# Norm factors of q and k as one power on GpSimd, and rope, factors and sums of squares over all four token blocks in one instruction

## The chip, the cores and the metric

The kernel runs on one core of a Trainium2 chip. The metric is device time in microseconds (us) of one execution. The engines are called by the short names of the profile: PE (TensorE, matrix products), PEld (its weight loads), DVE (VectorE), ACT (ScalarE), POOL (GpSimd) and SP (SyncE, which issues the DMAs here). They run at the same time, each with its own queue of instructions, in the order in which that queue was written.

## The reference

One block of a sparse-attention and recurrent network, followed by two layers of a second block. All arithmetic is in fp32, with 512 tokens and a width of 1024. What matters here is the second block: in each of its two layers four attention mixers read the same normed input, and each normalises its queries and keys head by head before the scores are formed.

```
def rms_norm(x, g):
    xf = x.astype(jnp.float32)
    y = xf * lax.rsqrt(jnp.mean(xf * xf, axis=-1, keepdims=True) + EPS)
    return (y * g.astype(jnp.float32)).astype(x.dtype)

def apply_rope(x, ang):
    x1, x2 = xf[..., :half], xf[..., half:]
    return jnp.concatenate([x1 * cos - x2 * sin, x1 * sin + x2 * cos], axis=-1)

# in each layer, between two feed-forward parts:
ya = neighbourhood_mixer(...)   # q, k: 4 heads of 64
yb = mla_mixer(...)             # q, k: 4 heads of 96 (64 plain + 32 with rope)
yc = diff_mixer(...)            # q, k: 8 halves of 32
yd = gqa_mixer(...)             # q: 4 heads of 64, k: 2 heads of 64, axial rope on both
x = x + jnp.concatenate([ya, yb, yc, yd], axis=-1) @ w_out[l]
```

The first block normalises the queries of its four head groups in the same way.

## The kernel before

Matrix products are done in three passes (L142 to L144, L172 to L174): each operand is split into a high and a low part, high by a copy on ACT (L125 for weights), low by a subtraction (L127 for weights, L225 for activations). In the attention stages the low part of the weights is made on POOL, elsewhere on DVE.

The program runs as one sequence of stages: the first block's attention and recurrence (`nsa`, about the first 500 us), feed-forward layers, the mixers of layer 0 (`mix`, about 1400 to 1740 us), feed-forward layers, the mixers of layer 1 (about 2460 to 2790 us), and a last feed-forward layer. Inside `mix` the sixteen heads run as a pipeline, in the order of mixers C (`diff`), A (`na`), D (`gqa`), B (`mla`): for head i the probabilities times values (`pv`), for head i+1 scores and softmax (`soft`), for head i+2 the transposes (`prep`). A filler (`Fill`) hands out the projections of the next mixer and the output products of earlier ones in small steps between these.

The final order on each engine is not that of the code: a scheduler with a simulated timeline orders the instructions by priority, and the steps of the filler have a lower one. Each engine then works through its queue strictly in order.

For q and k of a mixer the steps on the way from projection to transposes are:

- `proj` and `to` put the product into `tq` or `tk` (tokens on partitions, four blocks of 128 tokens side by side, `tb` is the block);
- `sums` (L677) squares it on ACT into a scratch tile `sqp` of 512 columns, of which there are two, and adds up each head on DVE (L683), one pair of instructions for each block;
- `factors` (L686) turns the sums of squares `hs` into reciprocal roots: with more than one head by `rstd_v` (L191), three Newton steps on DVE, with a single one by `rstd` (L182), one scaled sum on DVE and one power on POOL (L188);
- `bcm` (L699) multiplies q or k by the factors on DVE, block by block;
- `rope_n` (L690) makes two products with the tables on POOL (L693, L694) and adds the swapped halves of each 32 columns on DVE (L697), block by block; L1188 spreads the rotated part of `mla`'s k over the heads.

The names that return below: `hs` sums of squares, `nm` their scaled mean, `nt` the scratch of the Newton steps, `rq`, `rk` the factors, `sqp` scratch, `box` the q and k of `mla`, `ry` the factors of a mixer's output norm, `P` probabilities, `st` row statistics of the softmax, `PTl` the low part of the transposed probabilities, `nab` and `E` the bias of `na`.

Of the kernel before, what the change touches and what calls it, by code (L numbers as in the profile page):

```python
# [84 lines left out]
class Kern:  # L85
# [96 lines left out]
    def rstd(self, ss, width, n, tag, bufs=2):  # L182

        nc = self.nc
        m = self.sm.tile([128, n], FT, tag=tag + "m", name=tag + "m", bufs=bufs)
        nc.vector.tensor_scalar(m, ss, 1.0 / width, EPS, op0=OP.mult, op1=OP.add)
        r = self.sm.tile([128, n], FT, tag=tag, name=tag, bufs=bufs)
        nc.gpsimd.tensor_tensor(r, m, self.mhalf[:, :n], op=OP.pow)  # L188
        return r

    def rstd_v(self, ss, width, n, tag, bufs=2):  # L191

        V = self.nc.vector
        m, t = (self.sm.tile([128, n], FT, tag=c, name=c, bufs=2) for c in ("nm", "nt"))
        r = self.sm.tile([128, n], FT, tag=tag, name=tag, bufs=bufs)
        V.tensor_scalar(m, ss, 1.0 / width, EPS, op0=OP.mult, op1=OP.add)
        V.tensor_scalar(r.bitcast(I32), m.bitcast(I32), -0.5, 1597463007.0, op0=OP.mult, op1=OP.add)
        for _ in range(3):
            V.scalar_tensor_tensor(t, r, -0.5, r, op0=OP.mult, op1=OP.mult)
            V.tensor_mul(t, t, m)  # L200
            V.scalar_tensor_tensor(r, t, 1.5, r, op0=OP.add, op1=OP.mult)
        return r
# [426 lines left out]
    def mix(self, px, l, norm):  # L629
# [44 lines left out]
        def sqp():  # L674
            return tl("sqp", [128, T], FT, 2)

        def sums(t, n, d):  # L677

            ss = small("hs", [4, n], 4)
            for tb in range(4):  # L680
                sv = sqp()[:, :n * d].rearrange("p (h d) -> p h d", d=d)
                S.activation(sv, t[:, tb], AF.Square)
                V.tensor_reduce(ss[:, tb], sv, axis=AX, op=OP.add)  # L683
            return ss

        def factors(ss, n, d, tag):  # L686
            f = self.rstd_v if n > 1 else self.rstd
            return f(ss.rearrange("p t n -> p (t n)"), d, 4 * n, tag, 4).rearrange("p (t n) -> p t n", n=n)

        def rope_n(rope, t, tb, n, d):  # L690

            a = sqp()[:, :n * d].rearrange("p (h d) -> p h d", d=d)
# [183 lines left out]
        def diff():  # L876
# [19 lines left out]
            def projs():  # L896
                yield from proj(w_c[0], 256, to(q))
                rq = factors(sums(q8, 8, 32), 8, 32, "rq2")
                for tb in range(4):
                    bcm(q8[:, tb], rq[:, tb], 8, 32)  # L900
                yield from proj(w_c[1], 256, to(k))
                rk = factors(sums(k8, 8, 32), 8, 32, "rk2")
                for tb in range(4):
                    bcm(k8[:, tb], rk[:, tb], 8, 32)
                yield from proj(w_c[2], 256, lambda tb, ps, rt: vevac(Vt[:, tb], v4(ps), rt))
# [74 lines left out]
        def gqa():  # L980
            rope = tl("rope", [128, 2, 2, 4, 64])
# [14 lines left out]
            def post(t, n, i):  # L996
                th = t.rearrange("p t (h d) -> p t h d", d=64)
                f = factors(sums(th, n, 64), n, 64, "rq2")
                for tb in range(4):
                    bcm(th[:, tb], f[:, tb], n, 64)  # L1000
                    rope_n(rope[:, i], th[:, tb], tb, n, 64)
# [33 lines left out]
        def na():  # L1035
# [11 lines left out]
            def post(t):  # L1047
                th = t.rearrange("p t (h d) -> p t h d", d=64)
                f = factors(sums(th, 4, 64), 4, 64, "rq2")
                for tb in range(4):  # L1050
                    bcm(th[:, tb], f[:, tb], 4, 64)
# [78 lines left out]
        def mla():  # L1130
# [20 lines left out]
            def projs():  # L1151
# [33 lines left out]
                for tb in range(4):  # L1185
# [18 lines left out]
                for tb in range(4):  # L1204
                    bcm(qm[:, tb], rq[:, tb], 4, 96)
                    rope_n(rope[:, 0], qm[:, tb, :, 64:96], tb, 4, 32)
# [91 lines left out]
    def nsa(self, pa, pl, attnT, lru):  # L1298
# [176 lines left out]
        def post_q(g, t):  # L1475
# [6 lines left out]
            rq = self.rstd_v(ss, 64, 16, "rq")  # L1482
# [341 lines left out]
```

## Time and profile before

| | us |
|---|---|
| median of 3 runs | 3163.69 (3162.76 to 3170.32) |
| the profiled execution, its own time | 3163.88 |
| its span, first to last instruction | 3162.1 |
| PE busy in the span | 3041.4 (96%) |
| DVE busy | 1797.1 (57%) |
| ACT busy | 1396.7 (44%) |
| POOL busy | 686.8 (22%) |

The time of the profiled execution is 1.8 us above its span (what lies around the first and the last instruction) and 0.2 us above the median, so sums made in the trace can be read as sums of the median. Shares over the whole span are averages of stages that differ: in the feed-forward stages PE is busy without a gap and DVE about half of the time, while in the mixers DVE is nearly full. So the views that count here are those by stretch. A number in brackets behind a row of a timeline is the time that the engine sat idle before it, with the instruction that ended the wait.

### The profile page before, as it was taken

What the parts mean: (1) busy time and instruction counts of PE and PEld (TensorE: products, weight loads), DVE (VectorE), ACT (ScalarE), POOL (GpSimd) and SP (SyncE); (2) the same over time, 40 slices, a digit from 0 to 9 for tenths busy, and PEclk for the clock granted to TensorE, in tenths of its full rate; (3) what the DMA queues carried; (4) which work ended last, traced back from release to release, by engine and by line L of the source; (5) the groups of instructions that cost most, each with busy time, mean ns of one, the idle gap of its engine ahead of it and who ended that gap; (6) DMA issues with size and microseconds to landing.
All of it is one profiled execution on the core that took longest, in us unless ns stands there. A gap on an engine that the chain in (4) does not pass through costs nothing.

```text
span 3162.1 us, 41620 instructions
## 1 busy us (share of the span) xinstructions
PE 3041.4 (96%) x15289; PEld 2554.9 (81%) x15289; DVE 1797.1 (57%) x3520; ACT 1396.7 (44%) x2753; POOL 686.8 (22%) x746
## 2 busy tenths in 40 slices
PE   7999999999999999999888999999999998999998
PEld 6888777878888888888866888888888987778886
DVE  7677675454443444438886554354443698664433
ACT  4577674343332333336664333333332666543322
POOL 3366640010000000025752000010001566310000
PEclk9999999999999999999999999999999998999999
DMA  4221112333233233333201323323233322123332
GB/s 146 90 64 54 54 34 79 116 121 99 95 97 97 94 100 97 97 111 94 79 28 40 100 94 100 97 90 100 94 97 97 110 77 58 34 80 98 96 100 80
DMA packets 105268, 275.84 MB, mean 87 GB/s; under 512 B 27172, under 2 KB 36900, under 8 KB 104904
## 3 DMA queue, kind: packets, MB, share of 16 engines
q1 hardware_dynamic: 105064, 273.18, 27.8%
q8 instruction: 120, 1.97, 0.3%
q14 instruction: 84, 0.69, 0.1%
HBM read 268.93 MB, written 6.80 MB: 87 GB/s over the span
## 4 chain that ended last, share of the span: by engine, by line
PE 80%; DVE 10%; ACT 3%; POOL 2%; issue 2%; DMA 1%; SPq 0%; DVEq 0%; POOLq 0%; ACTq 0%
PE ps_mm L142 8%; PE ps_mm L144 8%; PE ps_mm L143 8%; PE ps_s L143 7%; PE ps_s L144 7%; PE ps_s L142 7%; PE ps_t L144 7%; PE ps_t L143 7%; PE ps_t L142 7%; PE ps_mm L172 2%; PE ps_mm L173 2%; PE ps_mm L174 2%; DVE PTl L225 1%; PE ps_t L1591 1%; DVE st L774 1%
## 5 line engine op out<-in xcount | busy, mean ns | idle before, releaser
L125 ACT ACTIVATE hi<-raw 128x512 fp32r<-128x512 f32 (+2 forms) x952 | 595.5, 627 | 1342.8 <-PE ps_mm L143 402.9
L127 DVE TENSOR_TENSOR lo<-raw,hi 128x512 fp32r<-128x512 f32 x782 | 543.6, 697 | 932.5 <-ACT hi L125 925.2
L142 PE MATMUL ps_mm<-xh,hi 128*128 128x512 f32 (+1 forms) x792 | 311.5, 394 | 2.8 <-ACT hi L125 2.3
L144 PE MATMUL ps_mm<-xh,lo 128*128 128x512 f32 (+1 forms) x792 | 309.7, 393 | 3.1 <-POOL lo L127 3.1
L143 PE MATMUL ps_mm<-xl,hi 128*128 128x512 f32 (+1 forms) x792 | 310.0, 391 | 0.0
L238 POOL TENSOR_TENSOR acc<-acc,sq 128x512 f32<-128x512 f32 x49 | 72.7, 1483 | 1056.4 <-ACT sq L236 529.4
L142 PE MATMUL ps_s<-xh,hi 128*128 128x512 f32 x656 | 253.2, 392 | 7.4 <-ACT hi L125 7.4
L143 PE MATMUL ps_s<-xl,hi 128*128 128x512 f32 x656 | 257.2, 392 | 2.3 <-DVE xl L243 2.1
L172 PE MATMUL ps_mm<-hi,xh 128*128 128x256 f32 (+1 forms) x896 | 256.2, 289 | 1.2 <-DVE gz L466 0.9
L144 PE MATMUL ps_s<-xh,lo 128*128 128x512 f32 x656 | 256.1, 391 | 0.0
L173 PE MATMUL ps_mm<-lo,xh 128*128 128x256 f32 (+1 forms) x896 | 255.1, 287 | 0.0
L127 POOL TENSOR_TENSOR lo<-raw,hi 128x512 fp32r<-128x512 f32 (+2 forms) x170 | 223.1, 1316 | 147.1 <-ACT hi L125 134.8
L174 PE MATMUL ps_mm<-hi,xl 128*128 128x256 f32 (+1 forms) x896 | 254.2, 287 | 0.1
L144 PE MATMUL ps_t<-xh,lo 128*128 128x512 f32 x608 | 236.3, 390 | 1.8 <-DVE lo L127 1.7
L142 PE MATMUL ps_t<-xh,hi 128*128 128x512 f32 x608 | 236.8, 390 | 0.0
L143 PE MATMUL ps_t<-xl,hi 128*128 128x512 f32 x608 | 236.6, 389 | 0.0
L144 PEld LDWEIGHTS ps_mm<-xh,lo 128*128 128x128 f32 (+1 forms) x792 | 148.7, 188 | 35.3 <-POOL lo L127 4.1
L142 PEld LDWEIGHTS ps_mm<-xh,hi 128*128 128x128 f32 (+1 forms) x792 | 148.9, 188 | 34.8 <-ACT hi L125 2.6
L172 PEld LDWEIGHTS ps_mm<-hi,xh 128*128 128x128 f32 x896 | 173.0, 194 | 3.1 <-DVE gz L466 1.1
L173 PEld LDWEIGHTS ps_mm<-lo,xh 128*128 128x128 f32 x896 | 173.2, 194 | 1.8 <-issue 0.4
L143 PEld LDWEIGHTS ps_mm<-xl,hi 128*128 128x128 f32 (+1 forms) x792 | 149.0, 188 | 30.6
L174 PEld LDWEIGHTS ps_mm<-hi,xl 128*128 128x128 f32 x896 | 172.1, 194 | 2.0 <-DVE xl L243 0.5
(540 smaller groups left out, 6714.4 us busy)
## 6 DMA issues: line engine op xcount, KB each, us to landing
raw<-in_w_g SPq DMA_DIRECT2D x110, 512.0 KB
raw<-in_w_u SPq DMA_DIRECT2D x110, 512.0 KB
raw<-in_w_d SPq DMA_DIRECT2D x108, 512.0 KB
raw<-in_w_o SPq DMA_DIRECT2D x24, 512.0 KB
raw<-in_w_c SPq DMA_DIRECT2D x16, 512.0 KB
raw<-in_w_m SPq DMA_DIRECT2D x16, 512.0 KB
raw<-in_w_a SPq DMA_DIRECT2D x12, 512.0 KB
raw<-in_w_d SPq DMA_DIRECT2D x20, 256.0 KB
```

Of the source, the lines that this page charges most:

```text
L125: nc.scalar.activation(hi[:, :c], x, AF.Copy)
L127: eng.tensor_tensor(lo[:, :c], x, hi[:, :c].bitcast(FT), op=OP.subtract)
L142: mm(ps, wh, mh(km), start=s, stop=False)
L143: mm(ps, wh, ml(km), start=False, stop=False)
L144: mm(ps, wl, mh(km), start=False, stop=e)
L172: mm(out[tb], h, wh, start=k == 0 and tb % 2 == 0, stop=False)
L173: mm(out[tb], h, wl, start=False, stop=False)
L174: mm(out[tb], o, wh, start=False, stop=k == K - 1 and tb % 2 == 1)
L225: self.nc.vector.tensor_sub(lo, src, hi.bitcast(FT))
L238: nc.gpsimd.tensor_tensor(acc, acc, sq, op=OP.add)
L774: V.tensor_reduce(mn, ps, axis=AX, op=OP.max, negate=True)
L1591: PE.transpose(tps[:, (qb - kb) * 128:(qb - kb + 1) * 128], P[qb][:, kb * 128:kb * 128 + 128], ident)
```

## The change

The Newton steps are gone: every factor comes from `rstd`, that is one scaled sum on DVE (L186) and one power on POOL (L188), whose width is the number of factors: 32 columns for `diff`'s q and k, 16 for those of `na`, for `gqa`'s q, `mla`'s q and k and the first block's q, 8 for `gqa`'s k. The scratch of the scaled sum becomes one tile name, `nm`, with four buffers for all callers. `sums`, `bcm` and `rope_n` work over as many token blocks at once as fit into 512 columns of scratch (`bcm` over all four).

```
     def rstd(self, ss, width, n, tag, bufs=2):
...
-        m = self.sm.tile([128, n], FT, tag=tag + "m", name=tag + "m", bufs=bufs)
+        m = self.sm.tile([128, 32], FT, tag="nm", name="nm", bufs=4)[:, :n]
         nc.vector.tensor_scalar(m, ss, 1.0 / width, EPS, op0=OP.mult, op1=OP.add)
         r = self.sm.tile([128, n], FT, tag=tag, name=tag, bufs=bufs)
         nc.gpsimd.tensor_tensor(r, m, self.mhalf[:, :n], op=OP.pow)
-        return r
-
-    def rstd_v(self, ss, width, n, tag, bufs=2):
-        V.tensor_scalar(m, ss, 1.0 / width, EPS, op0=OP.mult, op1=OP.add)
-        V.tensor_scalar(r.bitcast(I32), m.bitcast(I32), -0.5, 1597463007.0, op0=OP.mult, op1=OP.add)
-        for _ in range(3):
-            V.scalar_tensor_tensor(t, r, -0.5, r, op0=OP.mult, op1=OP.mult)
-            V.tensor_mul(t, t, m)
-            V.scalar_tensor_tensor(r, t, 1.5, r, op0=OP.add, op1=OP.mult)
         return r
...
         def sums(t, n, d):
...
-            for tb in range(4):
-                sv = sqp()[:, :n * d].rearrange("p (h d) -> p h d", d=d)
-                S.activation(sv, t[:, tb], AF.Square)
-                V.tensor_reduce(ss[:, tb], sv, axis=AX, op=OP.add)
+            s = max(i for i in (1, 2, 4) if i * n * d <= T)
+            for tb in range(0, 4, s):
+                sv = sqp()[:, :s * n * d].rearrange("p (h d) -> p h d", d=d)
+                S.activation(sv, t[:, tb:tb + s].rearrange("p t h d -> p (t h) d"), AF.Square)
+                V.tensor_reduce(ss[:, tb:tb + s].rearrange("p t h -> p (t h)"), sv, axis=AX, op=OP.add)
...
-        def rope_n(rope, t, tb, n, d):
-            G.tensor_tensor(a, t, rope[:, 1, tb, None, :].to_broadcast([128, n, d]), op=OP.mult)
-            G.tensor_tensor(t, t, rope[:, 0, tb, None, :].to_broadcast([128, n, d]), op=OP.mult)
-            for i in range(0, d, 32):
-                for u, v in ((i, i + 16), (i + 16, i)):
-                    V.tensor_add(t[:, :, u:u + 16], t[:, :, u:u + 16], a[:, :, v:v + 16])
+        def rope_n(rope, t, n, d):
+            s = max(i for i in (1, 2, 4) if i * n * d <= T)
+            for tb in range(0, 4, s):
+                x = t[:, tb:tb + s]
+                G.tensor_tensor(a.rearrange("p (t h d) -> p t h d", t=s, d=d), x,
+                                rope[:, 1, tb:tb + s, None, :].to_broadcast([128, s, n, d]), op=OP.mult)
+                G.tensor_tensor(x, x, rope[:, 0, tb:tb + s, None, :].to_broadcast([128, s, n, d]), op=OP.mult)
+                for u, v in ((0, 16), (16, 0)):
+                    V.tensor_add(x[..., u:u + 16], x[..., u:u + 16], a[..., v:v + 16])
 
         def bcm(t, f, n, d):
-            V.tensor_mul(t, t, f[:, :, None].to_broadcast([128, n, d]))
+            t = t.rearrange("p t h d -> p (t h) d")
+            V.tensor_mul(t, t, f.rearrange("p t h -> p (t h)")[:, :, None].to_broadcast([128, 4 * n, d]))
...
-                for tb in range(4):
-                    rope_n(rope[:, 1], kr[:, tb, None, :], tb, 1, 32)
-                    bcm(km[:, tb, :, 0:64], rk[:, tb], 4, 64)
-                    V.tensor_mul(km[:, tb, :, 64:96], kr[:, tb, None, :].to_broadcast([128, 4, 32]),
-                                 rk[:, tb, :, None].to_broadcast([128, 4, 32]))
+                rope_n(rope[:, 1], kr[:, :, None, :], 1, 32)
+                bcm(km[..., 0:64], rk, 4, 64)
+                V.tensor_mul(km[..., 64:96], kr[:, :, None, :].to_broadcast([128, 4, 4, 32]),
+                             rk[:, :, :, None].to_broadcast([128, 4, 4, 32]))
```

The callers lose their loops over `tb` in the same way (`diff`, `gqa`, `na`, q of `mla`), and `post_q` of the first block calls `rstd`. In all DVE issues 376 instructions fewer. No product of PE is added or taken away; since the scheduler orders anew, single instructions move by a few places on all engines in the attention stages. Line numbers of the changed kernel are lower: its L671, L694, L728, L768, L771, L772, L819 and L1177 are L683, L700, L734, L774, L777, L778, L825 and L1188 of before.

DVE, layer 0, the factors of `mla`'s k, before: the last of the three Newton steps (L199 to L201) and the first of four pairs of products, between row maxima (L774) and reciprocals (L777) of `gqa`'s softmax.

```order
L774 TENSOR_REDUCE st<-ps_s 128x1
L734 TENSOR_TENSOR qT<-ps_t,qT 64x512
L199 SCALAR_TENSOR_TENSOR nt<-rk_14837 128x16
L200 TENSOR_TENSOR nt<-nt,nm 128x16
L777 RECIPROCAL st<-st 128x1
L201 SCALAR_TENSOR_TENSOR rk_14837<-nt,rk_14837 128x16
L700 TENSOR_TENSOR box<-box,rk_14837 128x4x64
L1188 TENSOR_TENSOR box<-tk,rk_14837 128x4x32
```

The same place on DVE now, from the scaled sum (L186), behind which the power runs on POOL, to the two products that need it:

```order
L186 TENSOR_SCALAR nm<-hs 128x16
L768 TENSOR_REDUCE st<-ps_s 128x1
L771 RECIPROCAL st<-st 128x1
L671 TENSOR_REDUCE hs<-sqp 128x4
L728 TENSOR_TENSOR qT<-ps_t,qT 64x512
L819 TENSOR_TENSOR sq<-sq 128x512
L671 TENSOR_REDUCE hs<-sqp 128x4
L768 TENSOR_REDUCE st<-ps_s 128x1
L771 RECIPROCAL st<-st 128x1
L694 TENSOR_TENSOR box<-box,rk_14609 128x16x64
L1177 TENSOR_TENSOR box<-tk,rk_14609 128x16x32
```

Ten Newton instructions and eight products became two products, with other work between the scaled sum and them.

POOL at the same place, before: the probabilities of `gqa` are scaled (L778), with the factors of `na`'s output norm (`ry`) and the low parts of two weight tiles between.

```order
L778 TENSOR_SCALAR P<-P,st 128x512
L188 TENSOR_TENSOR ry<-rym,mhalf 128x4
L127 TENSOR_TENSOR lo<-raw,hi 128x512 x2
L778 TENSOR_SCALAR P<-P,st 128x512 x6
L127 TENSOR_TENSOR lo<-raw,hi 128x512 x2
```

And now, with the powers for `mla`'s k and q:

```order
L772 TENSOR_SCALAR P<-P,st 128x512
L188 TENSOR_TENSOR rk_14609<-nm,mhalf 128x16
L772 TENSOR_SCALAR P<-P,st 128x512 x2
L127 TENSOR_TENSOR lo<-raw,hi 128x512 x2
L772 TENSOR_SCALAR P<-P,st 128x512 x2
L188 TENSOR_TENSOR rq_14715<-nm,mhalf 128x16
L188 TENSOR_TENSOR ry<-nm,mhalf 128x4
L772 TENSOR_SCALAR P<-P,st 128x512
```

Two powers of 16 columns stand among the scalings of the probabilities, and `ry` now comes behind one of them.

## Rows read from the trace of the kernel before

**Rows 1.** The page, busy time by engine over the whole span.

```profile
PE 3041.4 (96%) x15289; PEld 2554.9 (81%) x15289; DVE 1797.1 (57%) x3520; ACT 1396.7 (44%) x2753; POOL 686.8 (22%) x746
```

**Rows 2.** Windows: stretch, length, busy PE, PEld, DVE, ACT, POOL; granted clock, DMA, GB/s.

```profile
0.00:500.00 500.00, 462.49 (x2669) 390.11 (x2670) 356.95 (x936) 325.22 (x741) 238.16 (x257) 0.96 0.22 72
1400.00:1435.00 35.00, 34.99 (x294) 34.78 (x293) 17.74 (x50) 16.59 (x35) 20.28 (x20) 1.00 0.41 124
1435.00:1650.00 215.00, 190.11 (x1279) 169.79 (x1276) 189.14 (x483) 146.07 (x348) 134.63 (x171) 0.94 0.24 69
2497.00:2710.00 213.00, 193.27 (x1257) 170.86 (x1255) 187.18 (x481) 146.04 (x347) 131.20 (x167) 0.92 0.22 65
```

**Rows 3.** Timeline of PE, layer 0: its two longest waits among the mixers.

```profile
1583.47 0.80 PE L1097 MATMUL ps_s<-kT,qT 128*128 128x256 f32 x2 [4.38 <-DVE st L1102]
...
1613.34 0.73 PE L792 MATMUL ps_o<-PTl,Vt 128*128 128x512 f32 x1 [4.81 <-DVE PTl L225]
```

**Rows 4.** Timeline of DVE ahead of the second of these waits.

```profile
1606.88 1.21 DVE L200 TENSOR_TENSOR nt<-nt,nm 128x16 f32<-128x16 f32 x1
...
1608.67 0.70 DVE L1188 TENSOR_TENSOR box<-tk,rk 128x128 f32<-128x128 f32 x1
...
1611.93 0.69 DVE L774 TENSOR_REDUCE st<-ps_s 128x1 f32<-128x512 f32 x1
...
1612.61 0.67 DVE L225 TENSOR_TENSOR PTl<-ps_t,PTh 128x512 fp32r<-128x512 f32 x1
```

**Rows 5.** Timeline of POOL ahead of both waits.

```profile
1582.23 2.09 POOL L1092 TENSOR_TENSOR nab<-namask,E 128x256 f32<-128x256 f32 x3 [4.18 <-issue]
...
1605.53 2.52 POOL L127 TENSOR_TENSOR lo<-raw,hi 128x512 fp32r<-128x512 f32 x2
```

**Rows 6.** Windows 1435:1650 and 2497:2710 summed, lines 197, 199, 200, 201, 700, 697, 683, 1188.

```profile
sum 428.00, DVE 3.58; mean DVE 1.79
sum 428.00, DVE 13.15; mean DVE 6.57
sum 428.00, DVE 15.78; mean DVE 7.89
sum 428.00, DVE 10.48; mean DVE 5.24
sum 428.00, DVE 24.09; mean DVE 12.04
sum 428.00, DVE 28.06; mean DVE 14.03
sum 428.00, DVE 25.47; mean DVE 12.74
sum 428.00, DVE 2.67; mean DVE 1.34
```

**Rows 7.** Groups of DVE by form: count, busy us, mean ns, idle before.

```profile
L1483 DVE TENSOR_TENSOR tq<-tq,rq 128x1024 f32<-128x1024 f32 x4 | 4.9, 1220 | 0.1
L1494 DVE TENSOR_TENSOR tk<-tk,rk 128x512 f32<-128x512 f32 x4 | 2.8, 711 | 0.0
L700 DVE TENSOR_TENSOR tk<-tk,rq 128x256 f32<-128x256 f32 x8 | 2.9, 421 | 0.1
L1481 DVE TENSOR_REDUCE ss<-tsq 128x8 f32<-128x512 f32 x8 | 5.5, 682 | 1.1 <-ACT tsq L1480 1.1
```

**Rows 8.** Groups of POOL by form: the power at 8, 4 and 1 columns.

```profile
L188 POOL TENSOR_TENSOR rk<-rkm,mhalf 128x8 f32<-128x8 f32 x4 | 6.6, 1649 | 16.2 <-DVE rkm L186 12.4 <-DVE st L1577 3.8
L188 POOL TENSOR_TENSOR rt<-rtm,mhalf 128x4 f32<-128x4 f32 x10 | 10.6, 1064 | 385.0 <-DVE rtm L186 385.0
L188 POOL TENSOR_TENSOR rc<-rcm,mhalf 128x1 f32<-128x1 f32 x1 | 0.6, 559 | 26.3 <-DVE rcm L186 26.3
```

**Rows 9.** Timelines of POOL and DVE: a power and a DVE instruction inside it.

```profile
344.40 1.65 POOL L188 TENSOR_TENSOR rk<-rkm,mhalf 128x8 f32<-128x8 f32 x1 [2.31 <-DVE st L1577]
...
344.65 0.69 DVE L499 SCALAR_TENSOR_TENSOR ti<-ti,xc 128x512 f32<-128x512 f32 x1 [0.27 <-ACT ti L496]
```

More of the change, by code (lines that the diff above doesn't have):

```diff
@@ L188, in rstd @@
         nc.gpsimd.tensor_tensor(r, m, self.mhalf[:, :n], op=OP.pow)
-        return r
-    def rstd_v(self, ss, width, n, tag, bufs=2):
-        V = self.nc.vector
-        m, t = (self.sm.tile([128, n], FT, tag=c, name=c, bufs=2) for c in ("nm", "nt"))
-        r = self.sm.tile([128, n], FT, tag=tag, name=tag, bufs=bufs)
-        V.tensor_scalar(m, ss, 1.0 / width, EPS, op0=OP.mult, op1=OP.add)
-        V.tensor_scalar(r.bitcast(I32), m.bitcast(I32), -0.5, 1597463007.0, op0=OP.mult, op1=OP.add)
-        for _ in range(3):
-            V.scalar_tensor_tensor(t, r, -0.5, r, op0=OP.mult, op1=OP.mult)
-            V.tensor_mul(t, t, m)
-            V.scalar_tensor_tensor(r, t, 1.5, r, op0=OP.add, op1=OP.mult)
         return r
@@ L684, in sums @@
             return ss
         def factors(ss, n, d, tag):
-            f = self.rstd_v if n > 1 else self.rstd
-            return f(ss.rearrange("p t n -> p (t n)"), d, 4 * n, tag, 4).rearrange("p (t n) -> p t n", n=n)
-        def rope_n(rope, t, tb, n, d):
-            a = sqp()[:, :n * d].rearrange("p (h d) -> p h d", d=d)
-            G.tensor_tensor(a, t, rope[:, 1, tb, None, :].to_broadcast([128, n, d]), op=OP.mult)
-            G.tensor_tensor(t, t, rope[:, 0, tb, None, :].to_broadcast([128, n, d]), op=OP.mult)
-            for i in range(0, d, 32):
-                for u, v in ((i, i + 16), (i + 16, i)):
-                    V.tensor_add(t[:, :, u:u + 16], t[:, :, u:u + 16], a[:, :, v:v + 16])
+            return self.rstd(ss.rearrange("p t n -> p (t n)"), d, 4 * n, tag, 4).rearrange("p (t n) -> p t n", n=n)
@@ new lines, in rope_n @@
+        def rope_n(rope, t, n, d):
+            s = max(i for i in (1, 2, 4) if i * n * d <= T)
+            for tb in range(0, 4, s):
+                x = t[:, tb:tb + s]
+                a = sqp()[:, :s * n * d]
+                G.tensor_tensor(a.rearrange("p (t h d) -> p t h d", t=s, d=d), x,
+                                rope[:, 1, tb:tb + s, None, :].to_broadcast([128, s, n, d]), op=OP.mult)
+                G.tensor_tensor(x, x, rope[:, 0, tb:tb + s, None, :].to_broadcast([128, s, n, d]), op=OP.mult)
+                x = x.rearrange("p t h (i c) -> p (t h) i c", c=32)
+                a = a.rearrange("p (h i c) -> p h i c", i=d // 32, c=32)
+                for u, v in ((0, 16), (16, 0)):
+                    V.tensor_add(x[..., u:u + 16], x[..., u:u + 16], a[..., v:v + 16])
@@ L898, in projs @@
                 rq = factors(sums(q8, 8, 32), 8, 32, "rq2")
-                for tb in range(4):
-                    bcm(q8[:, tb], rq[:, tb], 8, 32)
+                bcm(q8, rq, 8, 32)
                 yield from proj(w_c[1], 256, to(k))
                 rk = factors(sums(k8, 8, 32), 8, 32, "rk2")
-                for tb in range(4):
-                    bcm(k8[:, tb], rk[:, tb], 8, 32)
+                bcm(k8, rk, 8, 32)
                 yield from proj(w_c[2], 256, lambda tb, ps, rt: vevac(Vt[:, tb], v4(ps), rt))
@@ L998, in post @@
                 f = factors(sums(th, n, 64), n, 64, "rq2")
-                for tb in range(4):
-                    bcm(th[:, tb], f[:, tb], n, 64)
-                    rope_n(rope[:, i], th[:, tb], tb, n, 64)
+                bcm(th, f, n, 64)
+                rope_n(rope[:, i], th, n, 64)
             def projs():
@@ L1049, in post @@
                 f = factors(sums(th, 4, 64), 4, 64, "rq2")
-                for tb in range(4):
-                    bcm(th[:, tb], f[:, tb], 4, 64)
+                bcm(th, f, 4, 64)
             def projs():
@@ L1184, in projs @@
                 rk = factors(ss, 4, 96, "rk2")
-                for tb in range(4):
-                    rope_n(rope[:, 1], kr[:, tb, None, :], tb, 1, 32)
-                    bcm(km[:, tb, :, 0:64], rk[:, tb], 4, 64)
-                    V.tensor_mul(km[:, tb, :, 64:96], kr[:, tb, None, :].to_broadcast([128, 4, 32]),
-                                 rk[:, tb, :, None].to_broadcast([128, 4, 32]))
+                rope_n(rope[:, 1], kr[:, :, None, :], 1, 32)
+                bcm(km[..., 0:64], rk, 4, 64)
+                V.tensor_mul(km[..., 64:96], kr[:, :, None, :].to_broadcast([128, 4, 4, 32]),
+                             rk[:, :, :, None].to_broadcast([128, 4, 4, 32]))
                 w = self.stream(I["w_uq"][l], 2, 384)
@@ L1203, in projs @@
                 rq = factors(sums(qm, 4, 96), 4, 96, "rq2")
-                for tb in range(4):
-                    bcm(qm[:, tb], rq[:, tb], 4, 96)
-                    rope_n(rope[:, 0], qm[:, tb, :, 64:96], tb, 4, 32)
+                bcm(qm, rq, 4, 96)
+                rope_n(rope[:, 0], qm[..., 64:96], 4, 32)
             ys = ypair()
@@ L1481, in post_q @@
                 V.tensor_reduce(ss[:, i:i + 8], sq, axis=AX, op=OP.add)
-            rq = self.rstd_v(ss, 64, 16, "rq")
+            rq = self.rstd(ss, 64, 16, "rq")
             V.tensor_mul(qv, qv, rq[:, :, None].to_broadcast([128, 16, 64]))
```

## The prediction

> **What bounds the kernel now.** I read the busy times first: PE is busy for 3041.4 of 3162.1 us [rows 1], so all that can be won is some 120 us of idle PE, and what a lowered clock costs. No matrix product changes. The question is therefore where PE idles, and whether the removed DVE work is what it idles for.
>
> The view by stretch answers the first half [rows 2]. In the mixers of layer 0, 1435 to 1650 us, PE is busy 190.1 of 215 us, and its granted clock is 0.94 on average, that is 12% of the stretch at 1.2 GHz instead of 2.4. Six per cent of 215 is 12.9 us of PE work lost, so at full clock PE would need 190.1 - 12.9 = 177.2 us. DVE is busy for 189.1 us there (88%): it is the fuller of the two. Layer 1, 2497 to 2710 us, reads the same: PE 193.3 - 0.08 x 213 = 176.2 us at full clock, DVE 187.2 us of 213. Both stretches last some 26 us longer than their fuller engine is busy, since the two engines wait for each other in turn. In the first block's 500 us DVE has 71% and POOL 48%: less of a bound.
>
> The timeline shows how DVE holds PE up [rows 3]. PE waits 4.81 us for `PTl` at 1613.34 us. Ahead of it DVE worked through the last Newton step of `mla`'s k, four pairs of products and two reductions [rows 4]: steps of the filler that nobody needs at once, but they stand in the queue ahead of what PE needs. The other long wait, 4.38 us at 1583.47, has another root: POOL's bias step stood still for 4.18 us [rows 5], and behind it stands the load of the table `E`. The change does not touch that.
>
> **What goes from DVE.** In the two stretches together [rows 6]: the Newton steps (lines 197, 199, 200, 201) take 3.6 + 13.2 + 15.8 + 10.5 = 43.0 us and go entirely; the scaled sum ahead of them stays. The products with the factors (L700) take 24.1 us in 48 instructions. Six per layer remain: four of 1024 columns at 1.22 us, one of 512 at 0.71 and one of 1536, which by the step from 512 to 1024 is 1.73 us [rows 7], so 7.3 us per layer, 14.6 in all: 9.5 us less. The rope sums (L697) take 28.1 us in 96 instructions; ten per layer remain, at most 256 columns wide, at 0.42 us [rows 7]: 8.4 us, 19.7 less. The sums of squares (L683) take 25.5 us in 72; 17 per layer remain, none dearer than 0.68 us [rows 7]: at most 23.1 us, so at least 2.3 less. L1188: 2.7 us in eight become two at 0.71, 1.2 less. The sum is 43.0 + 9.5 + 19.7 + 2.3 + 1.2 = 75.7 us, 37.9 per layer. DVE falls to 151 us in layer 0 and to 149 in layer 1, below PE's 177 and 176.
>
> **What comes to POOL.** The power takes 0.56, 1.06 and 1.65 us at 1, 4 and 8 columns [rows 8], about 0.16 us per column. No row shows 16 or 32 columns. By the step they take 2.9 and 5.4 us; the ends are 1.65 us (no dearer than 8 columns) and twice or four times that, 3.3 and 6.6. I take the step. In each stretch five powers of 16 columns and one of 8 are added, 5 x 2.9 + 1.65 = 16.2 us. The rope products multiply as many columns as before in fewer instructions; I take them as unchanged. POOL goes from 134.6 to 151 of 215 us, 70%: not a bound by its load.
>
> The power also adds a wait to DVE: the product with the factors stands in DVE's queue and holds back all behind it, row maxima and `PTl` among it, until POOL is through. At `mla`'s k eight instructions now stand between the scaled sum and the product. With two row maxima at 0.69 us [rows 4] and two reductions they are some 4 us, which covers a power of 2.9 us if POOL takes it at once. At `mla`'s q and `gqa`'s q fewer stand between, and about 1 to 2 us of DVE stays open each time. Against 38 us less work I count that as covered by the room that DVE gains; if it is not covered, it belongs to the third case below.
>
> The Trainium skill speaks against this move: its page "GPSIMD Engine Reference", section "Key points", says that POOL shares its ways into SBUF with VectorE, and contends with DVE instructions of two SBUF inputs. The trace agrees for the subtraction on POOL, but not for the power; the rows stand with the fourth case.
>
> **Where it costs nothing.** The two powers of 32 columns (`diff`) fall to 1400 to 1435 us and its like in layer 1. PE is busy for 34.99 of 35 us there [rows 2], with projections that do not need them; POOL has 20.3 of 35 us and gets 10.8 more. The cover is the row of weight tiles already split; without it, up to 10.8 us per layer, since low parts of weights queue behind the powers. In the first block four Newton runs leave DVE and four powers of 2.9 us come to POOL, both below 75% there: I take 0, between a loss of 11.6 us (every power in the way) and a gain of the same size. ACT's squares become fewer and longer; ACT has 146 of 215 us [rows 2] and sets nothing.
>
> **The sum.** If each stretch keeps its 26 us above its fuller engine, it shrinks by the difference between DVE before and PE: 189.1 - 177.2 = 11.9 us in layer 0, 187.2 - 176.2 = 11.0 in layer 1. Together 22.9 us off 3163.9 us, the profiled execution's time, which stands 0.2 us from the median: **3141 us**. What is late next is PE itself, with the load of `E` and POOL's scaled probabilities. The ends: nothing comes back; or all idle and clock loss but the load of `E` (215 - 177.2 - 4.4 = 33.4 us in layer 0, 213 - 176.2 - 4.4 = 32.4 in layer 1 with the same kept), 66 us. I hold two thirds of that for the most that can be expected, 44 us, 3119 us.
>
> **The rivals.**
>
> *First case, the forecast.* DVE's room reaches PE: 3141 us, anywhere from 3119 to 3154. For it: 88% on DVE in both stretches, and rows such as those ahead of the 4.81 us wait. Chance 0.62.
>
> *Second case, the waits change their owner.* PE idles for chains, not for load: score, maximum, exponential, scaling on POOL, transpose. The Newton steps have a low priority and may mostly have filled gaps; the factors come no earlier through POOL (2.9 us and its queue against ten instructions of 0.2 to 0.4 us). Then only pile-ups such as the 4.81 us come back, some 4 us per layer less what the open waits on DVE take: 3160 us, between 3154 and 3173. For it speaks that no single wait of PE but that one is both long and DVE's. Chance 0.19.
>
> *Third case, slower: powers at the head of POOL's queue.* Two powers of `mla` now stand among the scalings of `gqa`'s probabilities, and PE's transposes wait for those. If every power were in PE's way, two layers would lose 2 x (16.2 + 10.8) = 54 us; it decides against the change from 22.9 / 54, when more than 42% of their time stands in PE's way. At two thirds it is 3163.9 - 22.9 + 36 = 3177 us. Against it: the scalings wait for DVE's reciprocals themselves, and POOL has 30% left. Chance 0.13.
>
> *Fourth case, the power holds DVE.* A Newton product of 16 columns took 1.21 us [rows 4] while POOL subtracted weights for 2.52 us [rows 5]; their mean over both stretches is 0.44 us (15.8 us over three steps of six runs in two layers, 36 instructions, [rows 6]). So POOL's wide subtractions do hold DVE. If powers held it too, 16.2 of the 37.9 us per layer would be lost again and I give half of the forecast: 3152 us. Against it: L499 on DVE, two SBUF inputs, took its 0.69 us inside a power of 1.65 us [rows 9]. Chance 0.06. This is the skill's rule above: by it the case holds, by rows 9 it does not.
>
> **How the numbers follow.** The likeliest case gives 3141 us. A difference below 0.3% (9.5 us) can't be told from no change. Faster by more than that: first and fourth case, 0.68. Within it: the second, 0.19. Slower: the third, 0.13. The range leaves out the third case and a little of the first case's lower end: 3118 to 3172 us; the first case's own is 3119 to 3154.
>
> **What would show it.** Right: in 1435 to 1650 us and its like DVE falls by 35 to 40 us, PE's idle time by about a third, the 4.81 us wait at `PTl` is gone, a power of 16 columns takes 2.5 to 3.3 us, and the feed-forward stages keep their lengths. Wrong: PE waits for transposes whose probabilities stand behind a power, DVE idles ahead of its products with the factors for more than some 10 us per layer, or a clock that stays low as often as before although DVE has room. The new order alone can also move pieces of a few us either way, which no row here can size.

## The result, and the profile after

The changed kernel takes 3131.1 us (median of 4 runs, 3130.5 to 3131.9) against 3163.2 us before: a ratio of 0.9894, 95% interval 0.9876 to 0.9911, or 32 us. The forecast was 3141 us, a gain of 22.9. The profiled execution of the changed kernel took 3131.08 us, its span 3129.3.

Where it went is told by a mark that each stage carries: the power on POOL that makes the norm factors `rt` of a layer's input. Before, it starts the mixers of layer 0 at 1405.8 us and the feed-forward stage behind them at 1747.3; the like marks of layer 1 are 2463.2 and 2800.8. After (timeline of POOL; start, duration, idle ahead in brackets):

```profile
1401.20 1.01 POOL L188 TENSOR_TENSOR rt<-nm,mhalf 128x4 f32<-128x4 f32 x1 [4.05 <-DVE nm L186]
...
1727.74 1.01 POOL L188 TENSOR_TENSOR rt<-nm,mhalf 128x4 f32<-128x4 f32 x1 [4.83 <-DVE nm L186]
...
2443.27 1.01 POOL L188 TENSOR_TENSOR rt<-nm,mhalf 128x4 f32<-128x4 f32 x1
...
2767.52 1.01 POOL L188 TENSOR_TENSOR rt<-nm,mhalf 128x4 f32<-128x4 f32 x1 [3.62 <-DVE nm L186]
```

So the mixers shrink from 341.4 to 326.5 us (-14.9) and from 337.6 to 324.3 us (-13.3). The first mixers are reached 4.6 us earlier, which the forecast did not have, and the feed-forward stages between keep their length (715.9 and 715.5 us).

The page's busy times [rows 1], and the windows of the two stretches, laid as far from the marks as those of [rows 2]; both are now 200 us long:

```profile
PE 3026.2 (97%) x15289; PEld 2544.2 (81%) x15289; DVE 1718.7 (55%) x3144; ACT 1390.1 (44%) x2707; POOL 763.6 (24%) x722
```

```profile
1430.00:1630.00 200.00, 184.24 (x1265) 165.27 (x1264) 158.32 (x342) 142.07 (x323) 152.64 (x156) 0.97 0.24 72
2477.00:2677.00 200.00, 187.32 (x1260) 167.13 (x1258) 158.58 (x345) 143.40 (x330) 151.49 (x153) 0.95 0.24 71
```

The first numbers are PE's: it idles 15.8 us of the first stretch where it idled 24.9, and 12.7 of the second where it idled 19.7; its granted clock is 0.97 instead of 0.94 and 0.95 instead of 0.92, so a part of the gain is clock. DVE (third) fell from 189.1 and 187.2 to 158.3 and 158.6 us, POOL (fifth) rose from 134.6 and 131.2 to 152.6 and 151.5.

PE's waits in layer 0, 1430 to 1632 us (total, times, longest): the long ones of [rows 3] are gone, the 4.81 us for `PTl` and also the 4.38 us behind POOL's bias step, which the change does not touch by itself. In the new order that step stands still for 1.50 us, until the load of `E` has landed, instead of 4.18.

```profile
PE ps_s L1087 <- DVE st L1092: 2.1, 3, 1.3
PE ps_o L785 <- ACT PTh L211: 1.6, 1, 1.6
PE ps_t L782 <- DVE kT L928: 1.2, 1, 1.2
PE ps_o L786 <- DVE PTl L212: 1.2, 2, 0.9
```

The power itself, by form, busy us and mean ns: as the step per column had it.

```profile
L188 POOL TENSOR_TENSOR rq<-nm,mhalf 128x16 f32<-128x16 f32 x12 | 34.9, 2905 | 3.0 <-DVE st L1565 2.7
L188 POOL TENSOR_TENSOR rq<-nm,mhalf 128x32 f32<-128x32 f32 x2 | 10.9, 5434 | 0.2
```

And what is left of the DVE lines of [rows 6] in the two stretches (windows 1430 to 1630 and 2477 to 2677 summed: the products with the factors L694, the rope sums L689, the sums of squares L671, L1177):

```profile
sum 400.00, DVE 19.48; mean DVE 9.74
sum 400.00, DVE 12.57; mean DVE 6.29
sum 400.00, DVE 21.18; mean DVE 10.59
sum 400.00, DVE 1.36; mean DVE 0.68
```

### The profile page after: what moved, and what is told of

Its sections match the earlier page's. It is cut to its first block, busy times and chain, and to the rows that moved or that the text cites. A ratio compares the mean times of both kernels' runs of the same rounds, so it can differ in the third digit from the quotient of the medians.

```text
span 3129.3 us, 41188 instructions
## 1 busy us (share of the span) xinstructions
PE 3026.2 (97%) x15289; PEld 2544.2 (81%) x15289; DVE 1718.7 (55%) x3144; ACT 1390.1 (44%) x2707; POOL 763.6 (24%) x722
## 3 DMA queue, kind: packets, MB, share of 16 engines
q8 instruction: 120, 1.97, 0.3%
## 4 chain that ended last, share of the span: by engine, by line
PE 71%; issue 13%; DVE 7%; POOL 4%; ACT 2%; DMA 1%; SPq 0%; DVEq 0%; POOLq 0%; ACTq 0%
PE ps_mm L142 8%; PE ps_mm L144 8%; PE ps_mm L143 8%; PE ps_s L143 6%; PE ps_s L144 6%; PE ps_s L142 6%; PE ps_t L144 6%; PE ps_t L143 6%; PE ps_t L142 6%; PE ps_mm L172 2%; PE ps_mm L173 2%; PE ps_mm L174 2%; POOL lo L127 1%; PE ps_t L1579 1%; DVE PTl L212 1%
```

## The experiments

All lengths between marks are those of one profiled execution each; for e2 that was the fastest of ten (3168.2 us), for e3 the slowest of ten (3162.5 us). The first block's column runs from the first `rt` power to the mark at the head of layer 0, and so holds the two feed-forward layers between too (721 us in every run).

| kernel | median us | ratio to before, 95% interval | first block | mixers 0 | mixers 1 |
|---|---|---|---|---|---|
| before | 3163.2 | | 1373.1 | 341.4 | 337.6 |
| after | 3131.1 | 0.9876 to 0.9911 | 1367.6 | 326.5 | 324.3 |
| e1 Newton, all blocks at once | 3148.3 | 0.9932 to 0.9962 | 1373.8 | 332.2 | 333.0 |
| e2 power, block by block | 3173.1 | 1.0017 to 1.0036 | 1367.2 | 346.6 | 341.3 |
| e3 power in the first block only | 3158.9 | 0.9975 to 0.9993 | 1369.2 | 340.8 | 340.9 |
| e4 after, Newton steps aside | 3146.3 | 0.9923 to 0.9956 | 1369.0 | 335.4 | 332.5 |
| e5 after, each power twice | 3178.9 | 1.0036 to 1.0066 | 1370.2 | 346.8 | 349.0 |
| e6 before, scratch renamed | 3166.2 | 0.9994 to 1.0013 | 1372.0 | 345.3 | 339.1 |
| e7 after, low parts shared | 3157.7 | 0.9976 to 0.9999 | 1383.8 | 330.7 | 332.0 |
| e8 after, factors by block | 3151.2 | 0.9948 to 0.9977 | 1369.0 | 333.5 | 337.7 |
| e9 after, product for power | 3115.6 | 0.9837 to 0.9866 | 1365.2 | 318.9 | 317.9 |
| e10 e2, product for power | 3140.8 | 0.9915 to 0.9944 | 1365.8 | 328.5 | 332.4 |
| e11 after, Newton for 32 columns | 3139.9 | 0.9909 to 0.9942 | 1370.1 | 331.8 | 327.5 |
| e13 after, filler later | 3141.9 | 0.9918 to 0.9951 | 1368.2 | 328.7 | 332.8 |

**What a difference must be to count.** Two runs size this. The first changes names and buffers and nothing else:

```diff
-        m = self.sm.tile([128, n], FT, tag=tag + "m", name=tag + "m", bufs=bufs)
+        m = self.sm.tile([128, 32], FT, tag="nm", name="nm", bufs=4)[:, :n]
...
-        m, t = (self.sm.tile([128, n], FT, tag=c, name=c, bufs=2) for c in ("nm", "nt"))
+        m, t = (self.sm.tile([128, n], FT, tag=c, name=c, bufs=2) for c in ("vm", "vt"))
```

> The kernel before with nothing but the scratch of the scaled sums renamed: one name with four buffers for all callers of the power, as in the changed kernel, and the Newton steps as they were. The instructions and, but for the names, their order on TensorE are those of before. It sizes what the renamed scratch does by itself: 3163 us with a difference below 0.1% if the name is nothing; anything else would be owed to buffers that come free at other times.

Its instructions stand in the order of before on all five engines. It stays at before (interval 0.9994 to 1.0013), though in its one profile the mixers of layer 0 are 3.9 us longer and start 1.5 us earlier: that much a single stretch moves by itself. The second gives the scheduler another order and no other work; the same edit stands at the filler of the first block, whose length hardly changes (1368.2 against 1367.6 us):

```diff
-        fill = Fill(lambda: tc.high_priority(offset=-300))
+        fill = Fill(lambda: tc.high_priority(offset=-1500))
```

> The changed kernel with one number changed that makes no work: the priority of the filler's steps in the mixers is lowered from -300 to -1500 against the rest, which gives the scheduler another order there (some 690 of 2391 rows of VectorE differ, 190 of 532 of GpSimd). It sizes what an order alone is worth. If the runs' differences of 10 us and more are made by what the instructions cost and not by where the scheduler happens to put them: 3127 to 3136 us. If the order alone is worth as much as the parts of the change: outside 3121 to 3141 us, and then no part of the change could be told by such runs.

3141.9 us: just outside the 3141 that I had set as the limit, 10.8 us above the changed kernel, 2.2 us of it in layer 0 and 8.5 in layer 1. So this one other order was worth 10.8 us, a third of what the change gave; whether a third order would be worth more is not known. By the expectation, runs that differ by no more than this cannot tell the parts of the change apart, and every other run here has an order of its own. So a difference of that size decides nothing, one of 15 to 20 us points somewhere without proving it, and I rest on the larger ones and on rows that show the mechanism.

**The two parts apart.** e1 keeps the Newton steps and takes the at-once form, e2 takes the power and leaves everything else block by block. e1 against after (the `rstd_v` of before and its scratch names are put back too):

```diff
...
-            return self.rstd(ss.rearrange("p t n -> p (t n)"), d, 4 * n, tag, 4).rearrange("p (t n) -> p t n", n=n)
+            f = self.rstd_v if n > 1 else self.rstd
+            return f(ss.rearrange("p t n -> p (t n)"), d, 4 * n, tag, 4).rearrange("p (t n) -> p t n", n=n)
...
-            rq = self.rstd(ss, 64, 16, "rq")
+            rq = self.rstd_v(ss, 64, 16, "rq")
```

and e2 against before (`rstd_v` goes, and the scratch is renamed as in e6):

```diff
...
-            f = self.rstd_v if n > 1 else self.rstd
+            f = self.rstd
...
-            rq = self.rstd_v(ss, 64, 16, "rq")
+            rq = self.rstd(ss, 64, 16, "rq")
```

> The after kernel with one part undone: the factors come from the eleven Newton steps on VectorE again, everywhere, while the rope, the products with the factors and the sums of squares stay over all blocks of tokens at once. Of the 75.7 us of VectorE work that the change takes out of the two mixer stretches by the forecast, this leaves out 43.0 (21.5 in each) and keeps 32.7. Load theory (what TensorE waits for in the mixers is an overbooked VectorE, whatever the work is): the gain of the mixers, 28.2 us between the marks, goes by VectorE time removed, so about 12 us of it stay, and the 4.6 us of the first block depend on which part made them; 3146 to 3152 us. Rival (the gain comes from the at-once instructions, which shorten the chains from a product to its transposes, and the Newton steps were hidden): 3131 to 3137 us. Rival (at-once is worth nothing by itself because its wide products take VectorE in longer pieces): about 3163 us.

> The before kernel with the other part alone: all factors by one power on GpSimd, while rope, products with the factors and sums of squares go block of tokens by block as before. VectorE loses the 43.0 us of Newton steps in the two mixer stretches and nothing else. Load theory: 16 us of the 28.2 of the mixers, and the first block's 4.6 if the power made them: 3142 to 3148 us. Rival (the Newton steps were hidden): about 3160 us. Rival (the power's latency stands in the way, 2.9 and 5.4 us against the chain of Newton steps, and only the at-once part makes up for it): above 3163 us.

e1 gains 14.9 us, nearly all of it in the mixers (9.2 and 4.6 us in its profile), and lies where the load theory had it. e2 misses that theory and lies where its last rival had it: it loses 9.9 us, although it reaches the mixers 6 us earlier. The parts don't add up: -15 and +10 alone, -32 together. The loss of 9.9 us is itself of the size of an order; what is clear of it is that the 15 to 21 us that the theory had for e2 did not come. By themselves the Newton steps out were no gain.

**The load by itself.** e4 leaves the changed kernel as it is and runs the Newton steps beside it, into tiles that nobody reads.

```diff
...
+            if n > 1:
+                newton_aside(ss.rearrange("p t n -> p (t n)"), d, 4 * n)
```

> The after kernel with the mixers' Newton steps put back on VectorE beside the power: the same eleven instructions on the same sums, into tiles that nothing reads, so that VectorE's load of before (43.0 us in the two stretches, 21.5 in each) returns while no chain gets longer by what it waits for. Nothing of what is computed changes. Load theory: about 16 of the 28.2 us of the mixers are lost, 3145 to 3149 us, and VectorE's busy time in each of the two stretches rises by some 21 us. Rival (what counts is the dependent chain from the sum to the transposes): within 4 us of the changed kernel, 3131 to 3135 us.

3146.3 us, 15.1 lost, where the load theory had it; in its profile the two mixers are 8.8 and 8.2 us longer, and DVE is busy for 177.0 of 209 us in layer 0, 18.7 more than in the 200 us of after. No chain got longer by what it waits for. Its loss is that of e1 (17.2 us above after) within the size that an order has. Two runs with different orders agree, so it is likely, though not proven, that given the at-once form what the Newton steps cost is mostly their time on DVE.

**Why the power alone lost.** First the power's time. e9 and e10 put a plain product in the place of every power of 16 or 32 columns, in the changed kernel and in e2:

```diff
-        nc.gpsimd.tensor_tensor(r, m, self.mhalf[:, :n], op=OP.pow)
+        nc.gpsimd.tensor_tensor(r, m, self.mhalf[:, :n], op=OP.mult if n > 8 else OP.pow)
```

> The changed kernel with every power of 16 or 32 columns replaced by a plain product of the same two operands on GpSimd: the same instruction count, tiles and waits, without the power's duration (the factors are then not the norm factors, which changes values and no sizes). Some 20 us of GpSimd per layer and 11 us in the first block go. The doubled power cost 47 of 54 added us. If a power's duration stands in TensorE's way as much when it is there once: 3095 to 3110 us. If the doubled one only passed a limit that the single one stays below: 3125 to 3133 us.

> The same replacement in the run with the power alone (rope, products with the factors and sums block by block). That run lost 10 us against the kernel before although VectorE was freed of the Newton steps. If the power's duration on GpSimd is what took that gain: 3138 to 3150 us. If it is the order, or the block-wise instructions of VectorE which wait one by one for the end of a GpSimd instruction: 3160 to 3175 us still.

The changed kernel with the product (e9: 0.22 us in the place of 2.91) is 15.6 us faster, 3115.6 instead of 3131.1, between the two expectations. Not all of this need be the power's duration: the scheduler ordered e9 anew as well, and some 640 of DVE's 3144 instructions stand in another place than after, against some 230 in e13, which moved 10.8 us. e10 is 32 us faster than e2, three times what e13's order was worth: with a cheap operation there e2 gains 22 us on before. And e5 runs each power of the mixers twice (`twice` is true for more than one head):

```diff
...
+        for _ in range(2 if twice else 1):
+            nc.gpsimd.tensor_tensor(r, m, self.mhalf[:, :n], op=OP.pow)
```

> The changed kernel with every power of the mixers that stands for several heads executed twice in a row on GpSimd, the second over the first; VectorE's work is the same. GpSimd gets 27 us more per layer (five powers of 2.9, one of 1.65, two of 5.4 us), and each factor comes 1.7 to 5.4 us later. Load theory with room on GpSimd: 3131 to 3138 us, a quarter of the added time at most. Rival (powers stand at the head of GpSimd's queue and in TensorE's way, the third case of the prediction): more than 42% of the added 54 us come back as time, 3154 us and more. The run of power by block lost some 5 us per layer against the kernel before; if the power's latency is the reason, this run must lose at least as much.

47.8 us lost, with POOL busy for 52.2 us more (815.8 against 763.6 on the pages): as the rival had it. POOL has room on average, but the powers stand at the head of its queue, and DVE, which works in order, stands behind them: between the marks it sits idle for factors of q and k for 13.6 us in layer 0 and 12.0 in layer 1, where after it does so for 1.7 and 0.2. The longest such row in e5's layer 0 (waits of DVE; total, times, longest):

```profile
DVE tk L696 <- POOL rk L189: 9.9, 1, 9.9
```

Second, what happens when the power ends. In e2 at 1470 us (timelines of POOL and DVE):

```profile
1467.12 2.91 POOL L188 TENSOR_TENSOR rq<-nm,mhalf 128x16 f32<-128x16 f32 x1
1469.99 1.30 POOL L127 TENSOR_TENSOR lo<-raw,hi 128x512 fp32r<-128x512 f32 x1
1471.26 1.46 POOL L943 TENSOR_SCALAR P<-P,std,nlam 128x512 f32<-128x512 f32 x1
1472.69 1.45 POOL L127 TENSOR_TENSOR lo<-raw,hi 128x512 fp32r<-128x512 f32 x1
...
1470.06 2.93 DVE L687 TENSOR_TENSOR tk<-tk,rq 128x256 f32<-128x256 f32 x4 [0.49 <-POOL rq L188]
```

The end of the power starts two instructions at once: POOL's next one, a wide subtraction, and 0.07 us later DVE's product, which reads two tensors from SBUF. The product is held until the subtraction ends. Four of them take 2.93 us here; before, at a moment when POOL was idle, the same four took 1.43 us:

```profile
1483.14 1.43 DVE L700 TENSOR_TENSOR tk<-tk,rq 128x256 f32<-128x256 f32 x4
```

That a DVE instruction is held to the end of one on POOL, however short it is itself, was to be read before: a Newton step of 16 columns took 1.21 us and ended 0.03 us after the subtraction beside it (1462.97 + 1.21 against 1462.88 + 1.27).

```profile
1462.97 1.21 DVE L200 TENSOR_TENSOR nt<-nt,nm 128x16 f32<-128x16 f32 x1
...
1462.88 1.27 POOL L127 TENSOR_TENSOR lo<-raw,hi 128x512 fp32r<-128x512 f32 x1
```

So the price is per instruction, and a product in one piece pays it once. After, at 1454.74 us:

```profile
1451.80 2.90 POOL L188 TENSOR_TENSOR rq<-nm,mhalf 128x16 f32<-128x16 f32 x1
1454.67 1.30 POOL L127 TENSOR_TENSOR lo<-raw,hi 128x512 fp32r<-128x512 f32 x1
1456.06 1.47 POOL L741 TENSOR_SCALAR qT<-qT 32x512 fp32r<-32x512 f32 x1
...
1454.74 2.31 DVE L694 TENSOR_TENSOR tq<-tq,rq 128x1024 f32<-128x1024 f32 x1
```

2.31 us where 1.22 was forecast: the 1.23 us from 1454.74 to the subtraction's end, and some 1.1 of its own. The hold runs the other way too: POOL's scaling `qT` at 1456.06 us started while the product ran and took 1.47 us, where the same took 0.61 at 1451.11 us. All six products of `tq` in each kernel (line views, 1380 to 2830 us; min, median and max ns) show that the power often brings the two together. Before, Newton in e1, then e2, after, and e9:

```profile
L700 DVE TENSOR_TENSOR tq<-tq,rq x24: 410/419/1536, 1417.0 to 2607.3; 128x256 f32<-128x256 f32 x24
```

```profile
L708 DVE TENSOR_TENSOR tq<-tq,rq x6: 1224/1226/1297, 1417.7 to 2584.0; 128x1024 f32<-128x1024 f32 x6
```

```profile
L687 DVE TENSOR_TENSOR tq<-tq,rq x24: 409/824/1516, 1415.3 to 2614.7; 128x256 f32<-128x256 f32 x24
```

```profile
L694 DVE TENSOR_TENSOR tq<-tq,rq x6: 1314/2198/2310, 1417.2 to 2587.3; 128x1024 f32<-128x1024 f32 x6
```

```profile
L694 DVE TENSOR_TENSOR tq<-tq,rq x6: 1211/1226/1482, 1407.9 to 2573.5; 128x1024 f32<-128x1024 f32 x6
```

Behind Newton steps the piece of 256 columns has a median of 419 ns, behind a power 824; the piece of 1024 columns 1226 behind Newton steps or a short product, 2198 behind a power. Not every product meets a subtraction: of the twelve of 1024 columns after (`tq`, `tk` and `box`), six start inside one and take 2.1 to 2.3 us, the others 1.2 to 1.5. All products with factors in both mixers together (1380 to 2830 us) take 31.9 us of DVE before, 20.4 in e1, 47.9 in e2, 37.0 in e10, 26.3 after, 21.2 in e9. So in e2 16 us came back on this line of the 43 saved on Newton steps, and 11 of the 16 go again with the power's duration (e10). Where the rest of the 32 us between e2 and e10 sits was not looked for.

e8 then undoes only that, in the changed kernel (over both mixers 64 products where there were 16):

```diff
-            t = t.rearrange("p t h d -> p (t h) d")
-            V.tensor_mul(t, t, f.rearrange("p t h -> p (t h)")[:, :, None].to_broadcast([128, 4 * n, d]))
+            for tb in range(4):
+                V.tensor_mul(t[:, tb], t[:, tb], f[:, tb, :, None].to_broadcast([128, n, d]))
```

> The changed kernel with the products with the factors (not the rope, nor the sums) block by block again: four of 256 columns where there was one of 1024, 36 instructions more. The long products took 1.97 us in the mixers where 1.22 was forecast, since GpSimd's wide products and subtractions run beside them. Load theory: VectorE's time changes by less than 3 us per layer, so 3129 to 3136 us. Rival (power and block-wise products go badly together, as the run with the power alone suggests, since the wait for the power then holds a row of instructions): a third to a half of the difference between that run and the changed kernel comes back, 3140 us and more. It tells whether the loss of that run sits in these products.

3151.2 us, as the rival had it: 20 us of the 42 between e2 and after, though by the sums just given, 31.9 us by block before and 20.4 at once in e1, the split would cost DVE 6 us per layer. The products take 52.9 us in it, twice the 26.3 of after. The other 22 us, the rope and the sums of squares by block, were not taken apart. One set of products (timelines of POOL and DVE): four, 4.67 us together, beside four subtractions. The first started ahead of them and took its 0.42 us; each of the next three was held by one and took 1.48 to 1.52.

```profile
1424.12 5.42 POOL L188 TENSOR_TENSOR rk<-nm,mhalf 128x32 f32<-128x32 f32 x1 [0.30 <-DVE nm L186]
...
1430.33 5.63 POOL L127 TENSOR_TENSOR lo<-raw,hi 128x512 fp32r<-128x512 f32 x4
...
1430.15 4.67 DVE L694 TENSOR_TENSOR tk<-tk,rk 128x256 f32<-128x256 f32 x4
```

**The first block.** e3 changes that place alone in the kernel before:

```diff
-            rq = self.rstd_v(ss, 64, 16, "rq")
+            rq = self.rstd(ss, 64, 16, "rq")
```

> The before kernel with the power in the first block's query factors alone (one head, eight powers of 8 columns); mixers and all later factors as before. The forecast has nothing for this place; the changed kernel reaches the first mixers 4.6 us earlier. If that comes from the power there: 3158 to 3160 us, with the start of the mixers near 1401 us instead of 1406. If it comes from the at-once form or from what follows in the order: 3163 us.

In the kernel as built these are four powers of 16 columns, one for each head group. The first mixers start 4.4 us earlier and the median falls by 4.4 us, as expected; e1, which lacks it, starts them only 0.4 us earlier. An order could make such a difference, so the rows count for more. They are DVE's, first of before, then of after: the product with the factors of one head group starts 2.41 us earlier, 2.0 us of it behind the scaled sum (147.11 and 146.71 us), since the Newton steps stood spread among the row maxima of that head group.

```profile
154.23 1.22 DVE L1483 TENSOR_TENSOR tq<-tq,rq 128x1024 f32<-128x1024 f32 x1
```

```profile
151.82 1.48 DVE L1471 TENSOR_TENSOR tq<-tq,rq 128x1024 f32<-128x1024 f32 x1
```

**Two attempts at a faster kernel.** e7 gives every third low part of the weights to DVE, e11 keeps the Newton steps for the two factors of 32 columns (`rstd_v` is put back).

```diff
 e7:
...
-                    eng = nc.gpsimd if self.attends else nc.vector
+                    self.los = self.los + 1
+                    eng = nc.gpsimd if self.attends and self.los % 3 else nc.vector
...
 e11:
...
+            f = self.rstd_v if 4 * n > 16 else self.rstd
```

> The changed kernel with every third low part of the weights in the attention stages made on VectorE instead of GpSimd. In each mixer stretch some 11 to 13 subtractions of 1.32 us leave GpSimd (15 us) and come to VectorE at about 0.7 us (8 us). If GpSimd's queue is what is late next: 3122 to 3128 us. Load theory with VectorE as the engine that counts: 8 of the 37 us come back on VectorE, so about 3 us per layer are lost, 3134 to 3140 us. If neither engine is a bound any more: 3131 us.

> The changed kernel with the Newton steps kept for the two factors of 32 columns of each layer (the first mixer's q and k, whose powers took 5.43 us each) and the power for all others. GpSimd loses 10.9 us per layer, VectorE gains twenty small instructions, some 5 to 9 us, at the start of the mixers where it is not full. If the long powers are in the way there: 3120 to 3128 us, the fastest of all. If VectorE's time counts wherever it falls: 3131 to 3138 us.

Both miss all that was expected of them. e7 loses 26.5 us, 16 of them in the first block; DVE now stands still at the head of its queue until ACT has made the high part (7.6 us in four waits in layer 0, 1430 to 1640 us). In the first 500 us these waits grew only from 21.0 to 26.7 us, so most of the first block's loss has no cause here. e11 is 8.8 us slower than after, which is within what an order is worth; it shows no gain from taking the long powers away. No kernel that computes all of the factors beat the changed one.

## Why the prediction was right, point by point

- **What bounds the mixers.** Right in kind: the waits that DVE ended shrank (the longest for `PTl` in layer 0 from 4.81 us to 0.9; all of PE's waits that DVE ended, between the marks, from 26.9 to 15.4 us in layer 0 and from 21.4 to 14.6 in layer 1), the feed-forward stages stayed, and DVE's load put back (e4) took 15 us away, where the mixers had gained 28. Another order was worth 10.8 us, so that figure is not exact.
- **What goes from DVE.** The Newton steps' 43.0 us went. The products with the factors saved 24.1 - 19.5 = 4.6 us, not 9.5: they were costed at 1.22 us, measured where no subtraction of POOL ran beside them, and take 1.97 us on average for q. The rope sums saved 28.1 - 12.6 = 15.5 us, not 19.7. The sums of squares saved 4.3 (forecast at least 2.3) and L1188 1.3. Together 68.7 us by these rows, not 75.7. DVE's busy time fell less still, by 376.3 - 316.9 = 59.4 us: rows that follow each other overlap in the record (a row of 0.69 us at 1454.01 us, the next at 1454.62), so that with 277 instructions less in the two stretches the busy time loses less than their durations add up to. I had set DVE to 151 and 149 us; it is 158 and 159, a fall of 30.8 and 28.6 us and not the 35 to 40 that were to be the sign.
- **What comes to POOL.** Sizes right: 2.9 and 5.4 us, POOL 152.6 us against 151.
- **The open wait on DVE, "covered by the room that DVE gains".** The wait itself is shorter than I had it: DVE sits idle for factors of q and k for 1.7 us in layer 0 and 0.2 in layer 1, where I had counted about 1 to 2 us each time. The sign of being wrong, 10 us per layer, did not come. What the prediction did not count is whatever else a power costs: e9 is 15.6 us faster, though DVE waits no less for factors there (1.9 and 0.7 us). How much of this is the power's duration and how much e9's order is not shown. If it were all duration, the mixers would pay 13.9 us for 48 us of power, 29%, below the 42% from which the third case would have decided; its own mechanism, scalings behind a power, is not seen after, since PE's waits that POOL ended stay as they were (3.7 us before, 3.4 after, both mixers). With every power twice (e5) the mixers are 45 us longer for 52 us more on POOL.
- **The mixers' sum.** 11.9 and 11.0 us forecast, 14.9 and 13.3 measured. The term that was mis-sized is the 26 us by which each stretch was to stay above its fuller engine. PE's need at full clock is 184.2 - 0.03 x 200 = 178.2 us and 187.3 - 0.05 x 200 = 177.3 us, as forecast; the stretches are 200 us, so 22 to 23 us remain, not 26. That the total came 9 us better than 3141 is within what an order is worth: with e13's order the same change takes 3141.9 us, so how close the sum came is in part luck.
- **The first block, costed at 0.** It gave 4.6 us (e3: 4.4). The bounds held it; the reason for 0, that DVE is below 75% there, was no reason: the rows show one head group's product waiting for one chain of steps.
- **Fourth case, the power holds DVE.** It does not: DVE instructions of two SBUF inputs inside a power take their usual time, as in [rows 9], and here 0.73 us within 2.91:

```profile
1470.04 0.73 DVE L949 SCALAR_TENSOR_TENSOR P<-P,std,P 128x512 f32<-128x512 f32 x1
...
1469.11 2.91 POOL L188 TENSOR_TENSOR rq<-nm,mhalf 128x16 f32<-128x16 f32 x1
```

  The Trainium skill's rule ("GPSIMD Engine Reference", "Key points": POOL contends with DVE instructions of two SBUF inputs) holds in this trace for POOL's wide two-input subtractions, not for the power. What the prediction missed is that the end of a power can start DVE's product beside POOL's next subtraction, so that the hold is paid once per product that meets one.

What stays open: how much of e9's 15.6 us is that hold (26.3 - 21.2 = 5.1 us of DVE time on the products), how much is factors and POOL's other work coming later, and how much is its order. No run separates them.

## What to carry to other kernels

Take the duration of an instruction from a place with the same neighbours: a DVE instruction with two SBUF inputs costs what POOL's instruction beside it still has to run, per instruction, so many small ones are dearer than their rows elsewhere say, and a step moved to POOL sets such meetings up by ending. When an edit has two parts, measure each alone: here one part gave nothing by itself (10 us lost, the size of an order) and 17 in the company of the other. And where a scheduler orders anew, run one reordering that changes no work before a difference of 0.3% is given a cause.

## What the runs showed that was not expected

- A DVE instruction held by POOL does its own work once POOL's instruction has ended: 16 columns ended 0.03 us behind it (1.21 us in all, at 1462.97 us before), 256 columns 0.28 us (1.48 in all, median of `tk<-tk,rk` in e2, against 0.42 before), 1024 columns 1.08 us (2.31 in all, at 1454.74 us after).
- The power, 1.6 to 3.3 us long at 8 and 16 columns, held none of the DVE instructions of 512 columns with two SBUF inputs that overlapped one in the mixers after: eight took 0.69 to 0.79 us.
- The same instructions in another order were worth 10.8 us (e13), more than some parts of the change.
